# Summed squares on VectorE, value products in pairs of key blocks, and downward blocks by token halves in a two-layer hybrid attention step

## The chip, the core and the metric

The kernel runs on one core of one Trainium2 chip. The metric is the time of one execution on the device in microseconds (us); lower is better. A core has five engines that run their own instruction streams side by side and wait for one another through semaphores: TensorE (PE in the profile, with its weight loads as PEld), VectorE (DVE), ScalarE (ACT), GpSimd (POOL) and SyncE (SP), whose stream here issues the weight transfers.

## The reference

One inference step of two trunk layers with a final norm, on 128 context tokens and 512 latent tokens of width 1024. Cut to what the change touches:

```
def rmsnorm(x, g):
    y = xf * lax.rsqrt(jnp.mean(xf * xf, axis=-1, keepdims=True) + EPS)
    return y * g
...
each layer:
    h   = rmsnorm(x) modulated by adaLN
    z   = h @ w_in                 -> differential, windowed and latent (MLA) heads
    p   = softmax(q k^T)           (context keys, then latent keys)
    mix = p @ v                    for every head
    x  += gate * (mix @ w_out)
    h   = rmsnorm(x) modulated by adaLN
    x  += gate * (relu(h @ w_up)^2 @ w_down)
final rmsnorm
```

The mean of squares of every token over its 1024 channels is what the first part of the change computes in another way; `p @ v` is the second part; the product with w_down the third.

## The kernel before

The activations lie transposed: xT holds 8 chunks of 128 channels by 640 tokens. The tokens go in two halves, HALVES = 0 to 256 and 256 to 640, that is 2 and 3 tiles of 128 (TILES). A product that must be exact is made of three matmuls of split operands, high by high, high by low and low by high (mm3, L540 to L544: lines L542, L543, L544). wh and wl are the high and low parts of a weight tile wr; ACT or DVE makes wh (L399, L414), DVE makes wl as a difference (L407).

The order of nearly all work is set by a planner, the class Plan. The code adds tasks with an engine, an estimated duration, the slots they read, write and allocate, and a priority; Plan schedules them against its own model of the engines (durations tA, tV, tP, hops HOP, ring sizes RINGS, and the settings KP of each layer with a sequence string), and emits each engine's instructions in that order. There are three plans: the attention of layer 0; the attention of layer 1, which begins with the last downward blocks of the MLP of layer 0; and the last downward blocks of layer 1 with the final norm. Between them stands the MLP of a layer, whose order is written out by hand as a list of blocks (L1725 onward): downward blocks ("d", product with w_down) and upward blocks ("u").

RINGS gives the number of buffers of each kind: E (scratch, four), PT (three), t (PSUM, three) matter here. A task that allocates from a full ring waits for the oldest holder's last reader.

The places that the change touches:

- stat(st, k, hf, prio), L639: ScalarE squares chunk k of token half hf into a buffer sq of ring E (L646); PE then multiplies each 128-token tile of it by a column of ones into the PSUM tile st (L651), adding up over the 8 chunks. The trace shows each of these f32 matmuls as two rows. rstd (L656 onward) turns st into the reciprocal root rsq (L611 to L623) and spreads it to all partitions (yb L665, rb L669). One round is all 8 chunks of both halves, 40 matmuls. There are five rounds: at the head of layer 0, in the third part of the output projection of each layer (the product with mix, 'po<-mix', whose residual L735 writes xT), and in the last downward blocks of each layer ('po<-Gt').
- quad(...), L986: two query tiles by two heads of one kind (sw, da, mla). Scores go to PSUM (sps; L1026 for mla), DVE takes the maximum (L1048), ACT the exponential (L1056). Then, per key block: four transposes of the probabilities (tr, L1095) into pt, one copy from PSUM to PT (ACT or DVE, as the planner chooses; lines L399 or L401), and the value product pv (L1099) into O. A value product is two matmuls, one for each head, with 64 columns each, so on half the width of the array.
- the block list, downs(g): for each pair of channel blocks mc two blocks, one for each channel block mi; a block makes the product of its channel block for both token halves, and the residual (L735) follows.
- KP of layer 1 has a key "split" that nothing reads.

pa<-wq,sc (L576) is the product of the conditioning vector with the adaLN weights; asb, pt (L581) its transposed result.

Of the kernel before, what the change touches and what calls it, by code (L numbers as in the profile page):

```python
# [15 lines left out]
ALU = mybir.AluOpType  # L16
# [3 lines left out]
P = 128  # L20
DEPTH = 2
D = 1024
KD = 8
# [4 lines left out]
HALVES = [(0, 256), (256, 640)]  # L28
# [14 lines left out]
N_CST = 900  # L43


RINGS = {"E": 4, "X": 5, "PT": 3, "B": 8, "h": 4, "mix": 3, "quad": 2, "QK": 4, "hs": 2, "wr": 3, "wh": 4, "wl": 4, "zin": 2, "sq4": 2,
         "stt": 10, "osb": 1, "Kc": 1, "ds": 2, "sm": 4, "rsq": 3, "Vsw": 1, "Vda": 1, "Vml": 1, "ckT": 1, "kz": 1,
         "s": 2, "t": 3, "o": 1, "z": 4, "T": 2, "ws": 2}

# [7 lines left out]
DMA0, DMAR = 2.0, 300e3  # L57
WINDOW = 3.413
N_PRE = 2

# [10 lines left out]
     "up_prio": 3500000.0, "split": "V", "evict": 999995.0, "resid": (4, 4, 8, 8), "half": 0.5,  # L71
     "seq": "s1 s0 c1 c2 s1 c1 s1 s1 c1 D0 c1 s0 c1 c1 c1 s0 s0 w1 c1 "
            "w0 d0 c1 D1 V0 c1 c1 c1 d0 d1 M0 d1 c1 w2 m0 m0 M1 m1 m1"},
]
# [7 lines left out]
def tV(n):  # L82
    return 0.07 + n / 960
# [281 lines left out]
def tile_hybrid_step(ctx: ExitStack, tc: tile.TileContext, i, o):  # L365
    nc = tc.nc
    V, S, G, T = nc.vector, nc.scalar, nc.gpsimd, nc.tensor
# [22 lines left out]
    def add(*a, **k):  # L390
        return cur[0].add(*a, **k)
# [43 lines left out]
    def sl(t, table, key):  # L435
# [11 lines left out]
    ones = sl(cst, CST, "ones")  # L447
# [18 lines left out]
                    in1=sil[:, 2].rearrange("p (k s) -> p k s", s=2), op=ALU.mult)  # L466
# [162 lines left out]
    def open_stats(ring, after=()):  # L629
        if ring == "s":  # L630
            x = mk(ring, [P, 2, 512], F32, "st")
            add("V", 0.1, lambda: V.memset(x.t[:, :, 0:4], 0.0), alloc=[x], prio=0.0, after=after)
            return [(x, lambda a, b, hf=hf: x.t[:, hf, a:b]) for hf in range(2)]
        st = [mk(ring, [P, 512], F32, "st") for _ in range(2)]
        for x in st:
            add("V", 0.1, lambda x=x: V.memset(x.t[:, 0:4], 0.0), alloc=[x], prio=0.0, after=after)
        return [(x, lambda a, b, x=x: x.t[:, a:b]) for x in st]

    def stat(st, k, hf, prio):  # L639

        a, b = HALVES[hf]
        w = b - a
        n = TILES[hf][1] - TILES[hf][0]
        x, view = st[hf]
        sq = mk("E", [P, NT], F32, "sq")
        add("A", tA(w) + 0.05, lambda: S.activation(out=sq.t[:, 0:w], in_=xT[:, k, a:b], func=AF.Square),  # L646
            r=[("x", (k, hf))], alloc=[sq], prio=prio)

        def mm():
            for t in range(n):  # L650
                T.matmul(out=view(t, t + 1), lhsT=sq.t[:, t * P:(t + 1) * P], rhs=ones,  # L651
                         start=False, stop=(k == KD - 1), skip_group_check=True)

        add("P", 0.115 * n, mm, r=[sq], w=[(x, hf)], prio=min(prio, 0.9e6))

    def rstd(st, hf, rb, prio):  # L656

# [328 lines left out]
    def quad(l, kind, u, hd, vt, vcols, mix, kt_mix, pr_, hs, at):  # L986
# [98 lines left out]
        ns = len(slots)  # L1085
        O = mk("o", [P, 256], F32, "O")
        p_t = PAR["tr"] + at
        for z, (kt, have) in enumerate(slots):
            pt, PT = mk("t", [P, 2, 256], F32, "pt"), mk("PT", [P, 2, 256], F32, "PT")
            c, w = have[0] * P, len(have) * P  # L1090

            def tr(pt=pt, kt=kt, have=have):
                for x in range(2):
                    for y in have:
                        T.transpose(pt.t[:, x, y * P:(y + 1) * P], e_.t[:, x, y, pos[y][kt]:pos[y][kt] + P], ident)  # L1095

            def pv(z=z, kt=kt, c=c, w=w, PT=PT):
                for x in range(2):
                    T.matmul(out=O.t[64 * x:64 * x + 64, c:c + w], lhsT=vt.t[:, kt, vcols[x]:vcols[x] + 64],  # L1099
                             rhs=PT.t[:, x, c:c + w], start=(z == 0), stop=(z == ns - 1))  # L1100

            add("P", 0.22 * len(have), tr, r=[(e_, (x, y)) for x in range(2) for y in have],
                alloc=[pt], prio=p_t)
            add("AV", {"A": tA(2 * w), "V": tV(2 * w)},
                lambda e, pt=pt, PT=PT, c=c, w=w: copy(e, PT.t[:, :, c:c + w], pt.t[:, :, c:c + w]),
                r=[pt], alloc=[PT], prio=PAR["evict"] + at)
            add("P", 0.255 * len(have), pv, r=[PT, (vt, kt)], w=[] if z == 0 else [O], alloc=[O] if z == 0 else [], prio=p_t,
                narrow=True)
        c0 = P + pr_ * 256
        if kind == "da":  # L1110
            osb = mk("osb", [P, 384], F32, "osb")
# [466 lines left out]
    for l in range(DEPTH + 1):  # L1578
# [134 lines left out]
        with ExitStack() as es:  # L1713
# [16 lines left out]
            def downs(g):  # L1730
                for mc in range(4):
                    if g < 7:
                        blocks.extend(("d", g, mc, mi, len(tiles)) for mi in range(2))
                    raws_.append(["d", g, mc, len(tiles)])
                    tiles.append([("d", g, mc)])

# [85 lines left out]
            for b_, blk in enumerate(blocks):  # L1822
# [1 line left out]
                wh, wl = wt[n_]  # L1824
                now, later = [], []
                if kind == "d":
                    g, mc, mi = f, q, x
                    m = mc * 2 + mi
                    mm_ = slice(mi * P, (mi + 1) * P)
                    whv, wlv = (z.rearrange("p (k n) -> p k n", k=4) for z in (wh, wl))  # L1830
                    for hf in range(2):
                        a0, b0 = HALVES[hf]
                        pu = bank()
                        for k in range(4):
                            gt = Gt[g][k // 2]
                            mm3(pu[:, :b0 - a0], (whv[:, k, mm_], wlv[:, k, mm_]),
                                (gt[:, 0, k % 2, a0:b0], gt[:, 1, k % 2, a0:b0]), k == 0, k == 3)
                        now.append(lambda m=m, hf=hf, pu=pu: emit_resid(l, 5, m, hf, pu))
                else:
                    if f // 4 not in Gt:  # L1840
                        Gt[f // 4] = [sp.tile([P, 2, 2, NT], R, tag="B", name="Gt", bufs=8) for _ in range(2)]
                    gt = Gt[f // 4][(f % 4) // 2]
                    z = {"A11": "X", "A12": "Y", "S2": "X", "S3": "Z", "S1": "X", "A22": "Z", "S4": "X"}[q]
                    new = q in ("A11", "A12", "S3")
                    if new:
                        banks[z] = bank()
                    pu = banks[z][:, 0:320]
                    whv, wlv = (t[:, 512 * x:512 * x + 512].rearrange("p (k n) -> p k n", k=4) for t in (wh, wl))
                    bh, bl = operand(q)
                    out = pu.rearrange("p (t n) -> p t n", n=64)  # L1850
                    for k in range(4):
                        for y, (w_, a_) in enumerate(((whv, bh), (whv, bl), (wlv, bh))):
                            T.matmul(out=out, lhsT=w_[:, k], rhs=a_[:, k], start=new and k == 0 and y == 0,  # L1853
                                     stop=k == 3 and y == 2, skip_group_check=True)
                    if q in ("A11", "S2", "S3"):
                        e = mp.tile([P, 384], F32, tag="X", name="pe", bufs=RINGS["X"])
                        banks["e" + q] = e
                        now.append(lambda e=e, pu=pu: copy(S, e[:, 0:320], pu))
                    else:
# [145 lines left out]
```

## Time and profile before

| | us |
|---|---|
| median of 3 runs | 1760.19 (1755.74 to 1761.95) |
| the profiled execution | 1761.53 |
| its span | 1759.8 |
| granted TensorE clock, mean | 0.984 |

The profile is one execution, read by the engine's rows: each has a start, a duration, the engine, the line, the operation with its output and inputs, and in brackets the idle time before it and what ended it. A busy row of PE can overlap the next, since matmuls are pipelined, so the cost of a stretch is read from start to start. The groups of the profile count the rows of all places of a line. A window view gives the busy time of each engine in a stretch of the span, then the granted clock, the share of the DMA engines and the GB/s. The parts of the program by time: the head to about 60 us, the attention of layer 0 to about 425, its output projection's last part and the entry to the MLP to about 500, the MLP to 870, its last downward blocks to 915; then the same for layer 1, and the final norm from about 1746.

### The profile page before, as it was taken

What the parts mean: (1) busy time and instruction counts of PE and PEld (TensorE: products, weight loads), DVE (VectorE), ACT (ScalarE), POOL (GpSimd) and SP (SyncE); (2) the same over time, 40 slices, a digit from 0 to 9 for tenths busy, and PEclk for the clock granted to TensorE, in tenths of its full rate; (3) what the DMA queues carried; (4) which work ended last, traced back from release to release, by engine and by line L of the source; (5) the groups of instructions that cost most, each with busy time, mean ns of one, the idle gap of its engine ahead of it and who ended that gap; (6) DMA issues with size and microseconds to landing.
All of it is one profiled execution on the core that took longest, in us unless ns stands there. A gap on an engine that the chain in (4) does not pass through costs nothing.

```text
span 1759.8 us, 29841 instructions
## 1 busy us (share of the span) xinstructions
PE 1676.2 (95%) x11335; PEld 1487.5 (85%) x11335; DVE 1242.9 (71%) x3229; ACT 809.5 (46%) x1798; POOL 199.5 (11%) x165
## 2 busy tenths in 40 slices
PE   7899999899899999999999999989889999999997
PEld 6687567568799999999998865857779999999997
DVE  3865778986868667766576767988577867766654
ACT  3532667774525333333254347777353433333321
POOL 0000001100013222212000000300001322212200
PEclk9999999999899999999999999999999999999999
DMA  9322553340122122222213244231111222222121
GB/s 314 102 84 87 200 165 96 108 139 25 61 70 87 61 87 82 97 85 77 89 52 98 88 135 137 90 108 56 36 61 50 71 93 76 96 88 70 61 73 61
DMA packets 67391, 163.24 MB, mean 93 GB/s; under 512 B 6896, under 2 KB 31280, under 8 KB 67248
## 3 DMA queue, kind: packets, MB, share of 16 engines
q1 hardware_dynamic: 67248, 161.34, 28.3%
q8 instruction: 90, 1.47, 0.3%
q14 instruction: 53, 0.43, 0.1%
HBM read 153.15 MB, written 8.16 MB: 92 GB/s over the span
## 4 chain that ended last, share of the span: by engine, by line
PE 79%; DVE 10%; ACT 4%; DMA 2%; issue 1%; POOL 1%; SPq 0%; DVEq 0%; ACTq 0%; POOLq 0%
PE pu L1853 18%; PE pu L543 8%; PE pu L542 8%; PE pu L544 8%; PE pt L1095 3%; PE O L1099 3%; PE po L542 3%; PE po L544 3%; PE pz L830 3%; PE pz L832 3%; PE po L543 3%; PE pz L831 3%; PE sps L1026 2%; PE st L651 2%; DMA zin<-zda 2%
## 5 line engine op out<-in xcount | busy, mean ns | idle before, releaser
L407 DVE TENSOR_TENSOR wl<-wr,wh 128x512 fp32r<-128x512 f32 (+2 forms) x290 | 287.0, 1010 | 62.0 <-ACT wh L414 37.4
L399 ACT ACTIVATE wh<-wr 128x512 fp32r<-128x512 f32 (+1 forms) x228 | 161.0, 736 | 282.6 <-PE pu L543 176.3
L542 PE MATMUL pu<-Gt,wh 128*128 128x384 f32 (+1 forms) x896 | 277.7, 310 | 5.1 <-DVE r L1449 5.1
L543 PE MATMUL pu<-Gt,wh 128*128 128x384 f32 (+1 forms) x896 | 277.6, 310 | 0.0
L544 PE MATMUL pu<-Gt,wl 128*128 128x384 f32 (+1 forms) x896 | 277.6, 310 | 0.0
L735 DVE SCALAR_TENSOR_TENSOR xT<-pu,ada,xT 128x128 f32<-128x128 f32 x336 | 134.8, 434 | 146.0 <-PE pu L544 145.7
L542 PEld LDWEIGHTS pu<-Gt,wh 128*128 128x128 f32 x896 | 170.6, 190 | 5.7 <-DVE r L1449 5.7
L543 PEld LDWEIGHTS pu<-Gt,wh 128*128 128x128 f32 x896 | 170.6, 190 | 0.0
L544 PEld LDWEIGHTS pu<-Gt,wl 128*128 128x128 f32 x896 | 170.5, 190 | 0.0
L1853 PE MATMUL pu<-Tl,wh 128*128 128x320 f32 x448 | 138.0, 308 | 0.0
L1853 PE MATMUL pu<-Th,wl 128*128 128x320 f32 x448 | 138.0, 308 | 0.0
L1853 PE MATMUL pu<-Th,wh 128*128 128x320 f32 x448 | 138.0, 308 | 0.0
L830 PE MATMUL pz<-wh,hh 128*128 128x512 f32 (+1 forms) x320 | 128.3, 401 | 2.1 <-DVE m L763 1.0
L831 PE MATMUL pz<-wl,hh 128*128 128x512 f32 (+1 forms) x320 | 123.4, 386 | 2.6 <-DVE wl L407 2.6
L735 DVE SCALAR_TENSOR_TENSOR xT<-po,ada,xT 128x128 f32<-128x128 f32 (+1 forms) x192 | 77.0, 434 | 66.3 <-PE po L544 65.2
L832 PE MATMUL pz<-wh,hl 128*128 128x512 f32 (+1 forms) x320 | 123.7, 386 | 0.1
L1048 DVE TENSOR_REDUCE stt<-sps 128x1 f32<-128x640 f32 (+2 forms) x160 | 116.1, 737 | 9.1 <-PE sps L1041 5.0
L1853 PE MATMUL pu<-hh,wh 128*128 128x320 f32 x336 | 104.2, 310 | 4.6 <-DVE r L1868 4.6
L1056 ACT ACTIVATE quad<-sps,stt 128x640 f32<-128x640 f32 (+2 forms) x128 | 91.2, 713 | 27.5 <-DVE stt L1048 26.9
L1853 PE MATMUL pu<-hh,wl 128*128 128x320 f32 x336 | 103.8, 309 | 0.0
L1853 PE MATMUL pu<-hl,wh 128*128 128x320 f32 x336 | 103.6, 308 | 0.0
L1427 POOL TENSOR_TENSOR xT<-xT,tm 128x256 f32<-128x256 f32 (+1 forms) x32 | 30.1, 941 | 619.8 <-ACT tm L1423 365.3
(313 smaller groups left out, 3930.7 us busy)
## 6 DMA issues: line engine op xcount, KB each, us to landing
wr<-in_w_ada SPq DMA_DIRECT2D x80, 512.0 KB, 3.8
wr<-in_w_up SPq DMA_DIRECT2D x64, 512.0 KB, 3.5
wr<-in_w_down SPq DMA_DIRECT2D x64, 512.0 KB, 3.5
wr<-in_w_in SPq DMA_DIRECT2D x24, 512.0 KB, 3.5
wr<-in_w_out SPq DMA_DIRECT2D x16, 512.0 KB, 4.5
wq<-in_w_ada SPq DMA_DIRECT2D x6, 1024.0 KB, 6.9
wr<-in_w_in SPq DMA_DIRECT2D x8, 416.0 KB, 3.4
xT<-in_xT SPq DMA_DIRECT2D x4, 640.0 KB, 7.1
```

The costliest lines, as they stand in the source:

```text
L399: S.activation(out=out, in_=in_, func=AF.Copy)
L407: eng.tensor_tensor(out=out, in0=a, in1=b, op=ALU.subtract)
L542: T.matmul(out=out, lhsT=w[0], rhs=a[0], start=first, stop=False)
L543: T.matmul(out=out, lhsT=w[0], rhs=a[1], start=False, stop=False)
L544: T.matmul(out=out, lhsT=w[1], rhs=a[0], start=False, stop=last)
L735: V.scalar_tensor_tensor(out=xT[:, m, a:b], in0=po[:, a - a0:b - a0], scalar=ada[l][:, sec, m, s:s + 1], in1=xT[:, m, a:b], op0=ALU.mult, ...
L830: T.matmul(out=out, lhsT=h_at(h, "h", k, tk), rhs=wh[:, x], start=(k == 0), stop=False)
L831: T.matmul(out=out, lhsT=h_at(h, "h", k, tk), rhs=wl[:, x], start=False, stop=False)
L832: T.matmul(out=out, lhsT=h_at(h, "l", k, tk), rhs=wh[:, x], start=False, stop=(k == KD - 1))
L1048: add("V", tV(we) - 0.01, lambda st=st, j=j, view=view: V.tensor_reduce(out=st.t[:, j:j + 1], in_=view(), axis=AX.X if kind == "sw" else A ...
L1056: S.activation(out=out, in_=view(), func=AF.Exp, bias=st.t[:, j:j + 1], accum_out=st.t[:, 4 + j:5 + j])
L1853: T.matmul(out=out, lhsT=w_[:, k], rhs=a_[:, k], start=new and k == 0 and y == 0, stop=k == 3 and y == 2, skip_group_check=True)
```

## The change

Four edits, in a kernel that is otherwise the same:

1. Summed squares: the squares of chunks 0 to 6 are added up by DVE in the buffer of chunk 0 (six adds per half and round), and PE multiplies by ones only that sum and the square of chunk 7: 10 matmuls a round in place of 40.
2. Value products: the transposes and copies of N_PV = 2 key blocks go first, then their value products as one task. Ring PT has four buffers in place of three. Five key blocks make groups of 2, 2 and 1.
3. Downward blocks by token halves: a block holds both channel blocks of a pair for one token half, in place of one channel block for both halves.
4. The unread key "split" goes.

```diff
-RINGS = {"E": 4, "X": 5, "PT": 3, ...
+RINGS = {"E": 4, "X": 5, "PT": 4, ...
...
+N_PV = 2
...
     def stat(st, k, hf, prio):
...
-        x, view = st[hf]
+        x, view, part = st[hf]
         sq = mk("E", [P, NT], F32, "sq")
         add("A", tA(w) + 0.05, lambda: S.activation(out=sq.t[:, 0:w], in_=xT[:, k, a:b], func=AF.Square),
             r=[("x", (k, hf))], alloc=[sq], prio=prio)
+        if k == 0:
+            part.append(sq)
+        elif k < KD - 1:
+            acc = part[0]
+            add("V", tV(w), lambda: V.tensor_tensor(out=acc.t[:, 0:w], in0=acc.t[:, 0:w], in1=sq.t[:, 0:w], op=ALU.add),
+                r=[sq], w=[acc], prio=prio)
+        if k < KD - 2:
+            return
+        src = part[0] if k < KD - 1 else sq
 
         def mm():
             for t in range(n):
-                T.matmul(out=view(t, t + 1), lhsT=sq.t[:, t * P:(t + 1) * P], rhs=ones,
+                T.matmul(out=view(t, t + 1), lhsT=src.t[:, t * P:(t + 1) * P], rhs=ones,
                          start=False, stop=(k == KD - 1), skip_group_check=True)
...
+            pvs.append((kt, c, w, PT))
+            if len(pvs) < N_PV and kt != slots[-1][0]:
+                continue
+
+            def pv(pvs=pvs, z0=z0, O=O):
+                for z, (kt, c, w, PT) in enumerate(pvs):
+                    for x in range(2):
+                        T.matmul(out=O.t[64 * x:64 * x + 64, c:c + w], lhsT=vt.t[:, kt, vcols[x]:vcols[x] + 64],
+                                 rhs=PT.t[:, x, c:c + w], start=(z0 + z == 0), stop=(z0 + z == ns - 1))
...
-                        blocks.extend(("d", g, mc, mi, len(tiles)) for mi in range(2))
+                        blocks.extend(("d", g, mc, hf, len(tiles)) for hf in range(2))
...
-                    g, mc, mi = f, q, x
-                    m = mc * 2 + mi
-                    mm_ = slice(mi * P, (mi + 1) * P)
+                    g, mc, hf = f, q, x
+                    a0, b0 = HALVES[hf]
...
-                    for hf in range(2):
-                        a0, b0 = HALVES[hf]
+                    for mi in range(2):
+                        m = mc * 2 + mi
+                        mm_ = slice(mi * P, (mi + 1) * P)
```

Since the planner works from the tasks, the order moves all over its three parts. Line numbers of the changed kernel are higher by 1 (helpers) to 19. Three places:

PE, the first instructions of the program, before; st is the sum of squares, pa the product with the conditioning vector, pt its transpose:

```order
L651 MATMUL st<-cst,sq 128x1 x37
L576 MATMUL pa<-wq,sc 32x128 x8
L651 MATMUL st<-cst,sq 128x1 x3
L581 MATMUL pt<-cst,asb 128x128
L576 MATMUL pa<-wq,sc 32x128 x8
```

and the same place of the changed kernel:

```order
L662 MATMUL st<-cst,sq 128x1 x10
L577 MATMUL pa<-wq,sc 32x128 x16
L680 MATMUL rb<-cst,yb 128x128 x2
L582 MATMUL pt<-cst,asb 128x128 x2
L577 MATMUL pa<-wq,sc 32x128 x8
```

All statistics now stand ahead of the first product with the conditioning vector, and the spread reciprocal root (rb) of the first half is two runs earlier.

PE, in the attention of layer 1, one group of latent attention (mla) before; quad are the probabilities, sps scores, spc scores of context queries:

```order
L1095 MATMUL pt<-cst,quad 128x128 x8
L1026 MATMUL sps<-Kml,Qml 128x320 x6
L1099 MATMUL O<-PT,Vml 64x256 x4
L1095 MATMUL pt<-cst,quad 128x128 x8
L1169 MATMUL spc<-Kcml,Qml 128x128 x6
L1099 MATMUL O<-PT,Vml 64x256 x4
L1095 MATMUL pt<-cst,quad 128x128 x4
```

and a group of the same kind in the changed kernel:

```order
L1107 MATMUL pt<-cst,quad 128x128 x8
L1037 MATMUL sps<-Kml,Qml 128x320 x6
L1107 MATMUL pt<-cst,quad 128x128 x4
L1121 MATMUL O<-PT,Vml 64x256 x4
L1107 MATMUL pt<-cst,quad 128x128 x8
L1037 MATMUL sps<-Kml,Qml 128x320 x6
L1121 MATMUL O<-PT,Vml 64x256 x6
```

Five key blocks have value products in runs of two and three blocks, with transposes of three blocks ahead of them; over the whole program the runs of value products on PE go from 90 to 53.

DVE, at the entry to the MLP of layer 0, before; Tl is the last sum of the normed tokens, r and Gt the first upward results, wl the low half of a downward weight tile, xT the residual of the first downward blocks:

```order
L407 TENSOR_TENSOR Tl<-hs,Th 128x4x384 x2
L407 TENSOR_TENSOR wl<-wr,wh 128x1024
L1449 SCALAR_TENSOR_TENSOR r<-pu,r 128x384 x4
L407 TENSOR_TENSOR Gt<-r,Gt 128x384 x4
L407 TENSOR_TENSOR wl<-wr,wh 128x1024 x3
L735 SCALAR_TENSOR_TENSOR xT<-pu,ada_92,xT 128x128 x2
```

and after:

```order
L408 TENSOR_TENSOR Tl<-hs,Th 128x4x384 x2
L1468 SCALAR_TENSOR_TENSOR r<-pu,r 128x384 x4
L408 TENSOR_TENSOR Gt<-r,Gt 128x384 x4
L408 TENSOR_TENSOR wl<-wr,wh 128x1024 x4
L746 SCALAR_TENSOR_TENSOR xT<-pu,ada_92,xT 128x128 x4
L746 SCALAR_TENSOR_TENSOR xT<-pu,ada_92,xT 128x384 x2
```

The first low half has moved behind the first upward results, and the residual goes by token halves.

More of the change, by code (lines that the diff above doesn't have):

```diff
@@ L43 @@
 N_CST = 900
-RINGS = {"E": 4, "X": 5, "PT": 3, "B": 8, "h": 4, "mix": 3, "quad": 2, "QK": 4, "hs": 2, "wr": 3, "wh": 4, "wl": 4, "zin": 2, "sq4": 2,
+RINGS = {"E": 4, "X": 5, "PT": 4, "B": 8, "h": 4, "mix": 3, "quad": 2, "QK": 4, "hs": 2, "wr": 3, "wh": 4, "wl": 4, "zin": 2, "sq4": 2,
          "stt": 10, "osb": 1, "Kc": 1, "ds": 2, "sm": 4, "rsq": 3, "Vsw": 1, "Vda": 1, "Vml": 1, "ckT": 1, "kz": 1,
@@ L70 @@
      "out": ("AV", "V"), "scale": "AV", "lead": 30, "prep": 950000.0, "tr": 900000.0, "up": ("A", "V"),
-     "up_prio": 3500000.0, "split": "V", "evict": 999995.0, "resid": (4, 4, 8, 8), "half": 0.5,
+     "up_prio": 3500000.0, "evict": 999995.0, "resid": (4, 4, 8, 8), "half": 0.5,
      "seq": "s1 s0 c1 c2 s1 c1 s1 s1 c1 D0 c1 s0 c1 c1 c1 s0 s0 w1 c1 "
@@ L632, in open_stats @@
             add("V", 0.1, lambda: V.memset(x.t[:, :, 0:4], 0.0), alloc=[x], prio=0.0, after=after)
-            return [(x, lambda a, b, hf=hf: x.t[:, hf, a:b]) for hf in range(2)]
+            return [(x, lambda a, b, hf=hf: x.t[:, hf, a:b], []) for hf in range(2)]
         st = [mk(ring, [P, 512], F32, "st") for _ in range(2)]
@@ L636, in open_stats @@
             add("V", 0.1, lambda x=x: V.memset(x.t[:, 0:4], 0.0), alloc=[x], prio=0.0, after=after)
-        return [(x, lambda a, b, x=x: x.t[:, a:b]) for x in st]
+        return [(x, lambda a, b, x=x: x.t[:, a:b], []) for x in st]
     def stat(st, k, hf, prio):
@@ L647, in stat @@
             r=[("x", (k, hf))], alloc=[sq], prio=prio)
+        if k == 0:
[7 more added lines that the diff above has]
+        src = part[0] if k < KD - 1 else sq
         def mm():
             for t in range(n):
-                T.matmul(out=view(t, t + 1), lhsT=sq.t[:, t * P:(t + 1) * P], rhs=ones,
+                T.matmul(out=view(t, t + 1), lhsT=src.t[:, t * P:(t + 1) * P], rhs=ones,
                          start=False, stop=(k == KD - 1), skip_group_check=True)
-        add("P", 0.115 * n, mm, r=[sq], w=[(x, hf)], prio=min(prio, 0.9e6))
+        add("P", 0.115 * n, mm, r=[src], w=[(x, hf)], prio=min(prio, 0.9e6))
     def rstd(st, hf, rb, prio):
@@ L1087, in quad @@
         p_t = PAR["tr"] + at
-        for z, (kt, have) in enumerate(slots):
+        z0, pvs = 0, []
+        for kt, have in slots:
             pt, PT = mk("t", [P, 2, 256], F32, "pt"), mk("PT", [P, 2, 256], F32, "PT")
@@ L1095, in tr @@
                         T.transpose(pt.t[:, x, y * P:(y + 1) * P], e_.t[:, x, y, pos[y][kt]:pos[y][kt] + P], ident)
[L1097 to L1100, printed above, removed]
             add("P", 0.22 * len(have), tr, r=[(e_, (x, y)) for x in range(2) for y in have],
@@ L1106, in quad @@
                 r=[pt], alloc=[PT], prio=PAR["evict"] + at)
-            add("P", 0.255 * len(have), pv, r=[PT, (vt, kt)], w=[] if z == 0 else [O], alloc=[O] if z == 0 else [], prio=p_t,
-                narrow=True)
+            pvs.append((kt, c, w, PT))
[6 more added lines that the diff above has]
+                                 rhs=PT.t[:, x, c:c + w], start=(z0 + z == 0), stop=(z0 + z == ns - 1))
+            add("P", 0.255 * sum(w // P for _, _, w, _ in pvs), pv,
+                r=[q for kt, _, _, PT in pvs for q in (PT, (vt, kt))], w=[] if z0 == 0 else [O],
+                alloc=[O] if z0 == 0 else [], prio=p_t, narrow=True)
+            z0, pvs = z0 + len(pvs), []
         c0 = P + pr_ * 256
```

## The prediction

> **What bounds the kernel now.** I read the page first: the busy shares, then the chain that ended last.
>
> ```profile
> span 1759.8 us, 29841 instructions
> ...
> PE 1676.2 (95%) x11335; PEld 1487.5 (85%) x11335; DVE 1242.9 (71%) x3229; ACT 809.5 (46%) x1798; POOL 199.5 (11%) x165
> ...
> PE 79%; DVE 10%; ACT 4%; DMA 2%; issue 1%; POOL 1%; SPq 0%; DVEq 0%; ACTq 0%; POOLq 0%
> ```
>
> TensorE (PE) is busy for 95% of the span and carries 79% of the chain. PE time that goes is mostly time that goes, unless another engine is late at that place. So I cut the span into stages; the columns are PE, weight load, VectorE, ScalarE and GpSimd busy us, then the granted clock.
>
> ```profile
> core 0: us, PE busy (x) PEld busy (x) DVE busy (x) ACT busy (x) POOL busy (x), PEclk, DMA share, GB/s
> ...
> 150.00:430.00 280.00, 263.34 (x1986) 187.56 (x1984) 206.64 (x587) 178.82 (x442) 17.46 (x24) 0.99 0.39 121
> ...
> 550.00:870.00 320.00, 320.00 (x2190) 320.00 (x2189) 218.69 (x394) 112.43 (x206) 61.98 (x43) 1.00 0.26 86
> 870.00:915.00 45.00, 45.00 (x302) 43.22 (x301) 28.37 (x87) 20.23 (x44) 0.00 (x0) 1.00 0.21 60
> ...
> 1713.00:1760.00 47.00, 36.90 (x270) 36.34 (x269) 22.38 (x69) 7.55 (x16) 0.00 (x0) 0.91 0.16 57
> ```
>
> In layer 0 the attention (150:430) has PE at 94%, the MLP (550:870) and the last downward blocks with the statistics of the next norm (870:915) have PE at 100% while VectorE has 32% and 37% of slack. Layer 1 repeats these stages, and 1713:1760 is its last downward stage and the tail.
>
> **The change part by part. 1, summed squares in the last downward stages.** A round (five tiles by eight chunks, 40 matmuls, each shown as two rows) falls to 10 matmuls, and there are five rounds, so the 400 rows of this group become 100.
>
> ```profile
> L651 PE MATMUL st<-cst,sq 128*128 128x1 f32 x400 | 57.0, 261 | 8.0 <-ACT sq L646 8.0
> ```
>
> What a set costs is read from start to start, since ends overlap.
>
> ```profile
> 878.01 0.50 PE L651 MATMUL st<-cst,sq 128*128 128x1 f32 x4
> 878.38 0.36 PE L542 MATMUL po<-Gt,wh 128*128 128x256 f32 x1
> 878.58 0.28 PE L543 MATMUL po<-Gt,wh 128*128 128x256 f32 x1
> 878.69 0.28 PE L544 MATMUL po<-Gt,wl 128*128 128x256 f32 x1
> ...
> 886.83 0.72 PE L651 MATMUL st<-cst,sq 128*128 128x1 f32 x6
> 887.41 0.42 PE L542 MATMUL po<-Gt,wh 128*128 128x384 f32 x1
> ```
>
> A set of two tiles holds PE for 0.37 us, and the product behind it is followed after 0.20 instead of 0.11: 0.46 us. Three tiles: 0.58 + 0.09 = 0.67. Six of eight sets go in each half: 6 x (0.46 + 0.67) = 6.8 us a round. In these two stages PE has no gap, so all of it counts: 2 x 6.8 = **-13.5 us**. [...]
>
> VectorE gains 6 adds per half. It has the same form, two f32 operands in SBUF, in these rows:
>
> ```profile
> 449.89 0.42 DVE L407 TENSOR_TENSOR hl<-hs,hh 128x256 fp32r<-128x256 f32 x1
> ...
> 471.72 0.55 DVE L407 TENSOR_TENSOR hl<-hs,hh 128x384 fp32r<-128x384 f32 x1
> ```
>
> 6 x (0.42 + 0.55) = 5.8 us a round. In 870:915 VectorE has 45.0 - 28.4 = 16.6 us free, which hides them. Without that cover they would be 11.6 us in the two stages, and the term would be -1.9. Bounds: -13.5 and -2.
>
> **2, the head.** The same sets stand at the very start.
>
> ```profile
> 7.58 15.95 PE L651 MATMUL st<-cst,sq 128*128 128x1 f32 x74 [7.58 <-ACT sq L646]
> 23.45 1.08 PE L576 MATMUL pa<-wq,sc 128*32 128x128 f32 x16
> 24.46 1.44 PE L651 MATMUL st<-cst,sq 128*128 128x1 f32 x6
> 25.77 0.45 PE L581 MATMUL pt<-cst,asb 128*128 128x128 f32 x1
> ```
>
> The waits of the first 60 us (total us, times, longest), and a window of the same stretch:
>
> ```profile
> DVE rsq L611 <- PE st L651: 20.8, 2, 19.5
> ...
> 32.00:40.00 8.00, 7.80 (x49) 4.74 (x50) 4.65 (x17) 2.79 (x7) 0.00 (x0) 1.00 0.92 310
> ```
>
> 80 rows end at 25.8, 0.215 us each (the first 74 in 15.95), and the reciprocal root (rsq) waits for them 19.5 us. After, 20 rows cost 4.3 us, and the squares set the pace: 16 squares and 12 adds in turns. ScalarE alone needs 16 x 0.47 = 7.5 us from 7.1, to 14.6; squares and adds strictly in turn need 7.5 + 5.8 more, to 20.4; ring E has four places, of which the two sums hold two. I take 18. PE then has 8 us less in front of the projections. But up to 40 us the transfers run at 92% or more, and the wq loads on SP's queue wait for the pa products that are moved forward; what PE does at 33 cannot all come 8 us sooner. I take **-5**, between 0 (transfers bind) and -10.
>
> **3, the two output projections.** Their third parts run at 425:448 and 1268:1291.
>
> ```profile
> 440.00:448.00 8.00, 8.00 (x60) 8.00 (x60) 4.51 (x15) 3.56 (x6) 0.00 (x0) 1.00 0.21 68
> 448.00:456.00 8.00, 7.71 (x61) 5.91 (x59) 7.97 (x24) 7.56 (x21) 0.00 (x0) 1.00 0.37 131
> ...
> 464.00:472.00 8.00, 2.58 (x10) 1.51 (x10) 5.85 (x17) 4.66 (x11) 0.00 (x0) 0.75 0.00 1
> 472.00:480.00 8.00, 7.75 (x30) 7.68 (x30) 8.00 (x16) 5.49 (x11) 0.00 (x0) 0.61 0.01 2
> ```
>
> To 448 PE is full and VectorE has 44% free; from 448 VectorE is full and PE stands for 5.4 us of 464:472. The first piece would give 6.8 us. But the 5.8 us of adds come just ahead of a stretch in which VectorE binds, and behind an add wait the residual of the next block, the normed halves (hs, hl) and PE's upward products. I take **-3 a stage, -6** in all; bounds -6.8 and +5.8 a stage, so -13.6 and +11.6.
>
> **4, value products two key blocks at a time.** The matmuls stay; what goes is changes between full and half width of the array.
>
> ```profile
> 395.98 1.05 PE L1026 MATMUL sps<-Kml,Qml 96*128 96x320 f32 x6
> 396.86 1.04 PE L1095 MATMUL pt<-cst,quad 128*128 128x128 f32 x8
> ...
> 400.57 1.12 PE L1026 MATMUL sps<-Kml,Qml 96*128 96x320 f32 x6
> 401.62 1.08 PE L1099 MATMUL O<-PT,Vml 128*64 128x256 f32 x8
> 402.63 0.66 PE L1095 MATMUL pt<-cst,quad 128*128 128x128 f32 x4
> ...
> 404.33 0.65 PE L1099 MATMUL O<-PT,Vml 128*64 128x256 f32 x4
> 404.91 0.45 PE L542 MATMUL po<-mix,wh 128*128 128x384 f32 x1
> ```
>
> Into the run: six scores hold PE 0.88 us ahead of transposes, 1.05 ahead of a value product, 0.17 more. Out: four rows take 0.58, eight 1.01, so 0.43 for four and 0.15 fixed. One trip costs 0.32 us. By the order of the instructions PE makes 53 such runs instead of 90: 37 x 0.32 = 11.8 us. The price is a wait: the first block's evicted copy now waits for the second's.
>
> ```profile
> L399 ACT ACTIVATE PT<-pt 128x512 f32<-128x512 f32 (+1 forms) x91 | 51.1, 575 | 31.9 <-PE pt L1095 29.2 <-PE O L1099 2.0
> ```
>
> An eviction takes 0.58 us, and PE can go on only with what stands between. In the new order mostly other work stands there (six scores, 0.9 us, or products), and ring PT has a fourth place, so that two pairs are under way. Priced with such rows, 20 of 144 gaps between a last transpose and its value product were shorter than 1.2 us before, and 6 are now. The planner also reorders the whole stage: ten value evictions go from VectorE to ScalarE, and some scalings to VectorE. PE has 17 us of gaps in 150:430 that may grow or shrink; I bound this reshuffle at +20 over both layers. I take **-9**, bounds -12 and +8.
>
> **5, downward blocks by halves, and the entry to the MLP.** A block has the same 24 matmuls with four forms in another order; PE at 100% in 550:870 does the same work, so 0. At the entry of layer 0 the order changes.
>
> ```profile
> 491.14 1.23 DVE L407 TENSOR_TENSOR wl<-wr,wh 128x1024 fp32r<-128x1024 f32 x1 [3.13 <-ACT wh L414]
> 492.29 1.94 DVE L1449 SCALAR_TENSOR_TENSOR r<-pu,r 128x384 f32<-128x384 f32 x4
> 494.15 1.95 DVE L407 TENSOR_TENSOR Gt<-r,Gt 128x384 fp32r<-128x384 f32 x4
> ...
> 494.28 0.39 PE L542 MATMUL pu<-Gt,wh 128*128 128x256 f32 x1 [2.54 <-DVE r L1449]
> ```
>
> Before, the low half of the first weight (wl) was made ahead of r and Gt. After, it stands behind both on VectorE: 491.1 + 1.9 + 1.9 + 1.2 = 496.1 if r starts at once, and up to 497.3 if not, and PE's third matmul needs it, which before could go at about 494.7, right behind the last row and the one after it. That is +1.6 to +2.8; I take +2.6. In layer 1 the order stays and the first products need one token half only: 0 to -2, I take -1. Sum **+1.6**.
>
> **The sum.** -13.5 - 5 - 6 - 9 + 1.6 = -31.9 on the profiled execution's 1761.5: 1729.6. That execution is 1.3 above the median, so 1728. Bounds: all at best -13.5 - 10 - 13.6 - 12 - 0.4 = -49.5, 1711; all at worst -1.9 + 0 + 11.6 + 8 + 2.8 = +20.5, 1781, which needs every cover to fail at once.
>
> **Rivals.** *VectorE takes PE's place* in the head and in the output projections: the adds there are as long as the sets (5.8 against 6.8). For it: 7.97 of 8 us busy at 448:456. Against it: 44% free just before. Then the stages give 0 and the head 0: -13.5 - 9 + 1.6 = -21, and with +3 a stage -15: 1742 to 1745.
>
> *PE falls to half rate more often.* In 472:480, behind a gap of 5.4 us, the granted clock is 0.61. With sets of matmuls gone, PE is left with gaps. Such a fall costs 8 x (1 - 0.61) = 3.1 us; four more (each output projection, the head, the start of an attention) cost 12.4: 1728 + 12 = 1740. Against it: where the most matmuls go, PE is gapless. [...]
>
> *The change doesn't do what it says:* the planner spends the PE time that goes in gaps elsewhere, and the total stays at 1755 to 1765. Against it: 13.5 us lie where PE has no gap.
>
> *Slower: value products wait for the second eviction.* Place: transposes and value products of both attentions. If less than 0.9 us of PE work stands between the last transpose of a pair and its products, PE waits out the hop and the 0.58 us. At 80 pairs of four-row transposes, 80 x 0.6 = 48 us, against savings of 33: +15, 1775. It decides from 55 such pairs on (33/0.6); the order shows 6 short gaps, but evictions that stand behind other work on ScalarE or VectorE would count too.
>
> **How the numbers follow.** Forecast 0.70 (1728, own range 1716 to 1738); VectorE in PE's place 0.12 (1742 to 1745); half rate 0.10 (1740); no change 0.04 (1760); slower 0.04 (1775). The range takes the forecast's lower bound, 1711, and reaches to 1749 over both middle rivals. A measurement of this kernel tells 0.3% (5.3 us) from no change. Faster 0.92, same 0.04, slower 0.04.
>
> **What would show each step.** 1: 100 rows of st<-cst,sq, the last downward stages 6 to 7 us shorter with PE still at 100%; a wait of PE on adds there refutes it. 2: the wait of rsq on st down from 19.5 to about 12, PE's projections 5 us sooner. 3: the span from the last part of the output projection to the first upward product 3 us shorter, and no more than 8 us idle behind it. 4: 37 fewer runs of value products, PE waits on PT not above the 6 or so us of before. 5: PE's first downward product at layer 0 waits on wl. The forecast is wrong if PE's total falls by 25 us or more but the span does not.

## The result and the profile after

The changed kernel takes 1709.63 us (median of 4 runs, 1707.87 to 1710.98) against 1759.93 before (4 runs): a ratio of 0.9717, 95% interval 0.9696 to 0.9737, so 50.3 us less. The forecast was 1728 with a range from 1711 to 1749: the sign was right, the size too small by 18 us, and the range missed the time by 1.4 us. Medians and ratios here and below leave out two executions, one of pairs with three buffers and one of the kernel before in another order (j3), which took 2684 and 2690 us at a granted clock of 0.56.

The profiled execution took 1707.87 us, 53.7 less than that of before; it lies 1.8 below its median, that of before 1.6 above. The page of the changed kernel, the lines that answer to those of before:

```profile
span 1706.1 us, 29317 instructions
...
PE 1617.0 (95%) x11035; PEld 1446.2 (85%) x11035; DVE 1276.6 (75%) x3293; ACT 801.9 (47%) x1792; POOL 203.8 (12%) x167
...
PE 75%; DVE 14%; ACT 5%; DMA 2%; issue 2%; POOL 1%; DVEq 0%; SPq 0%; ACTq 0%; POOLq 0%
```

PE is busy 59 us less at the same share of the span, and VectorE's share of the last chain went from 10% to 14%. To see where the time went, I cut both traces at the same points of the program, read off PE's rows: the first product of each input projection (pz), the first upward block of each MLP that reads the token sums (Tl, Th), and the first of the last downward blocks (po<-Gt). The windows view of before, the seven stages in order (head, attention 0, MLP 0, last downward 0, attention 1, MLP 1, last downward 1; an attention stage includes the output projection and the entry to the MLP):

```profile
0.00:33.61 33.61, 23.99 (x152) 20.86 (x153) 8.85 (x47) 12.70 (x27) 0.20 (x4) 1.00 0.97 330
33.61:527.56 493.95, 462.38 (x3141) 361.72 (x3138) 360.93 (x1139) 271.53 (x650) 25.50 (x30) 0.98 0.34 106
527.56:867.62 340.06, 338.05 (x2307) 337.52 (x2306) 237.01 (x414) 122.41 (x228) 74.44 (x50) 1.00 0.25 85
867.62:904.10 36.48, 36.48 (x269) 36.48 (x269) 22.90 (x66) 17.86 (x39) 0.00 (x0) 1.00 0.13 38
904.10:1371.01 466.91, 438.91 (x2896) 355.67 (x2896) 351.01 (x1081) 253.92 (x610) 25.20 (x31) 0.97 0.27 85
1371.01:1711.60 340.59, 338.04 (x2306) 337.52 (x2305) 238.87 (x414) 122.47 (x228) 74.15 (x50) 1.00 0.23 79
1711.60:1753.17 41.57, 38.30 (x278) 37.74 (x277) 20.05 (x62) 8.61 (x17) 0.00 (x0) 0.98 0.11 39
```

and of the changed kernel:

```profile
0.00:24.76 24.76, 10.64 (x93) 8.45 (x94) 13.80 (x57) 11.93 (x28) 0.20 (x4) 1.00 0.99 329
24.76:503.49 478.73, 445.59 (x3077) 355.19 (x3077) 370.46 (x1159) 266.51 (x644) 25.34 (x30) 0.98 0.35 116
503.49:843.84 340.35, 338.21 (x2307) 337.69 (x2305) 238.92 (x414) 122.48 (x228) 74.63 (x50) 1.00 0.25 85
843.84:873.13 29.29, 29.29 (x203) 29.25 (x203) 23.93 (x70) 16.06 (x35) 0.93 (x2) 1.00 0.11 33
873.13:1320.63 447.50, 421.66 (x2841) 345.39 (x2840) 361.19 (x1099) 253.69 (x614) 28.56 (x31) 0.99 0.29 90
1320.63:1662.92 342.29, 339.75 (x2306) 339.22 (x2305) 239.85 (x414) 122.58 (x228) 74.14 (x50) 1.00 0.23 78
1662.92:1699.47 36.55, 31.83 (x218) 30.99 (x217) 25.23 (x74) 8.61 (x17) 0.00 (x0) 0.96 0.12 43
```

The second number is the stage's length, the third PE's busy time. Head -8.9; last downward stages -7.2 and -5.0; MLPs +0.3 and +1.7; the two attention stages **-15.2 and -19.4**. The forecast had -5, -13.5 together, 0, and -13.4 for both attention stages. So the error lies mostly in the attention stages: 34.6 us where 13.4 were forecast.

A stage's length has three parts: gaps (length less PE's busy time), what PE loses to the granted clock (busy time by one less the clock, summed over windows of 1 us; called half rate below), and the rest, its **work** in full-speed time. The windows view gives a clock of 1.00 also where the trace has no record of it, and the record begins only at 37.9 us in before and at 23.8 in the changed kernel. By its rows, PE ran at about half speed ahead of it: the first projection rows of before follow one another at 0.43 us, and those behind 38 us at 0.23.

```profile
34.20 0.63 PE L831 MATMUL pz<-wl,hh 128*128 128x512 f32 x1
34.63 0.63 PE L832 MATMUL pz<-wh,hl 128*128 128x512 f32 x1
...
39.96 0.39 PE L830 MATMUL pz<-wh,hh 128*128 128x512 f32 x1
40.19 0.39 PE L831 MATMUL pz<-wl,hh 128*128 128x512 f32 x1
```

So I take a clock of 0.5 up to the first record, an estimate from these rows. By the view alone the attention stages of before would have 2.1 us more work and as much less half rate; it is 1.0 to 2.1 in the other runs whose head keeps its 40 matmuls, and nothing in the rest. For the two attention stages together: work 879.1 to 856.5, **-22.6**; half rate 22.2 to 10.8, **-11.4**; gaps 59.6 to 59.0, -0.6. The work that left is closer to the undiscounted prices of the prediction, 2 x 6.8 for the sums and 11.8 for the pairs, 25.4, than to the 15 that it counted. The rest is less time at half rate, which the prediction had counted as 0. Each split is of one execution: those of the kernel before beside the last set lay between 1752.7 us at a granted clock of 0.990 and 1761.8 at 0.984, so a few us of half rate belong to the execution.

### The profile page after: what moved, and what is told of

It is laid out like the page before. It is cut to its first block, busy times and chain, and to the rows that moved or that the text cites. A ratio compares the mean times of both kernels' runs of the same rounds, so it can differ in the third digit from the quotient of the medians.

```text
span 1706.1 us, 29317 instructions
## 1 busy us (share of the span) xinstructions
PE 1617.0 (95%) x11035; PEld 1446.2 (85%) x11035; DVE 1276.6 (75%) x3293; ACT 801.9 (47%) x1792; POOL 203.8 (12%) x167
## 4 chain that ended last, share of the span: by engine, by line
PE 75%; DVE 14%; ACT 5%; DMA 2%; issue 2%; POOL 1%; DVEq 0%; SPq 0%; ACTq 0%; POOLq 0%
PE pu L1872 18%; PE pu L545 8%; PE pu L544 8%; PE pu L543 8%; PE pt L1107 3%; PE po L543 3%; PE pz L841 3%; PE O L1121 3%; PE pz L842 3%; PE pz L843 3%; PE po L544 3%; PE po L545 3%; DVE stt L1059 2%; DVE wl L408 2%; DMA zin<-zda 1%
## 5 line engine op out<-in xcount | busy, mean ns | idle before, releaser
L408 DVE TENSOR_TENSOR wl<-wr,wh 128x512 fp32r<-128x512 f32 (+2 forms) x290 | 291.6, 1027 | 55.5 <-ACT wh L415 31.0
L408 DVE TENSOR_TENSOR Gt<-r,Gt 128x320 fp32r<-128x320 f32 (+2 forms) x128 | 79.0, 624 | 25.2 <-ACT Gt L400 25.2
L408 POOL TENSOR_TENSOR wr<-wr 128x512 f32<-128x512 f32 x28 | 39.4, 1407 | 486.0 <-DMA wr<-in_w_up 345.2
## 6 DMA issues: line engine op xcount, KB each, us to landing
wq<-in_w_ada SPq DMA_DIRECT2D x6, 1024.0 KB, 12.1
```

Source lines behind the costliest of these rows:

```text
L408: eng.tensor_tensor(out=out, in0=a, in1=b, op=ALU.subtract)
```

## The experiments

Theories: **A**, prices: each matmul and each change of array width that leaves PE counts in full. **B**, VectorE binds in the output projections, and what went beyond the forecast comes from the planner's new order. **C**, the fourth PT buffer, not the pairs, makes the second part. The times below are medians; the kernel before, run beside each set, had 1757.8, 1758.1, 1758.0 and 1756.1, so a comparison across sets is good to some 4 us. Orders of one kernel, shown last, differ by up to 6 us in work, so a smaller difference of work tells nothing by itself.

### The parts alone

The summed squares alone: the stat hunk of the diff on the kernel before.

```diff
+            add("V", tV(w), lambda: V.tensor_tensor(out=acc.t[:, 0:w], in0=acc.t[:, 0:w], in1=sq.t[:, 0:w], op=ALU.add),
```

> The summed squares alone, on the kernel before. Theory A (prices add up: every set of sums that leaves PE counts in full, in the head, in both output projections and in both last downward stages): head -9, output projections 2 x -6.8, last downward stages 2 x -6.8, some -36 us, about 1724. Theory B (the extra gain of the changed kernel comes from the planner's new order, which needs the pairs of value products or their fourth buffer): head -9, downward stages -13, output projections near -3 each, about 1732. The entry to the attention stages decides: from the first product of the input projection to the first upward block of the MLP, -6.8 a layer by A, about -3 a layer by B.

Measured 1716.9, ratio 0.9766 (0.9751 to 0.9780), -40.9. More than either theory. Work in the attention stages fell by 14.6 (A: 13.6), gaps and half rate by 10.3.

The pairs alone: the quad hunks with N_PV = 2 and PT at 4.

```diff
-"PT": 3
+"PT": 4
...
+N_PV = 2
...
```

> Value products of two key blocks and the fourth PT buffer alone, on the kernel before. Runs of value products on PE fall from 92 to 53. Theory A (0.32 us a trip, no waits): -12 us, 1748, all in the two attention stages. Theory B (the new order of the whole stage brings more than the trips): -20 us or more. Theory C (it does nothing without the relief of PE and VectorE by the other part): within 5 us of before.

Measured 1738.7, ratio 0.9894 (0.9879 to 0.9908), -19.2. Work in the attention stages fell by 11.2 (A: 12), gaps by 3.0, half rate by 8.0. The price of a trip was about right, and the time moved by more, nearly as far as B has it. The trace of before has 92 runs of value products, not the 90 counted ahead of the prediction: 39 trips less, 12.5 us by the price.

The downward blocks by halves alone:

```diff
-blocks.extend(("d", g, mc, mi, len(tiles)) for mi in range(2))
+blocks.extend(("d", g, mc, hf, len(tiles)) for hf in range(2))
...
```

> Downward blocks by token halves alone, on the kernel before. All theories: the MLP blocks cost the same; A expects 0 to -3 us at the two entries to the MLP, B allows for -5 and more where the first half's block no longer waits for the second half's upward results.

Measured 1758.3, ratio 1.0006 (0.9992 to 1.0019): nothing, work unchanged at 879.1.

The two parts together, without the third (the hunks of both, downs as before):

```diff
+N_PV = 2
...
+            add("V", tV(w), lambda: V.tensor_tensor(out=acc.t[:, 0:w], in0=acc.t[:, 0:w], in1=sq.t[:, 0:w], op=ALU.add),
...
```

> Summed squares and pairs of value products without the downward blocks by halves. A: -36 - 12 = -48, about 1712, the changed kernel less than 3 us faster. B: the parts don't add up, and this differs from the sum of the two single parts by more than 6 us.

Measured 1708.9, ratio 0.9730 (0.9713 to 0.9746), -48.9, the changed kernel's time. The single parts sum to -60.1, 11.2 more, so in time they don't add up. By work in the attention stages they nearly do, 14.6 + 11.2 = 25.8 against 22.1, a difference that orders alone can make; gaps and half rate don't: 10.3 + 11.0 = 21.3 against 11.2.

### The output projections

The sums everywhere but in the output projections:

```diff
...
-                        stat(sts, m, hf_, 0.2e6 + m)
+                        stat(sts, m, hf_, 0.2e6 + m, each=True)
```

> The kernel before with the summed squares in the head and in the last downward stages only; the third part of both output projections keeps 40 matmuls a round. Against the run with summed squares everywhere (-41 us), the difference is the term of the output projections. Theory A (each set that leaves PE counts in full there too): 13.6 us and what the half-rate spells of PE change with it, so -41 + 14 = -27, about 1731. Theory B (VectorE takes PE's place there, as the prediction's discount has it): 6 us, -35, about 1723.

Measured 1742.4, ratio 0.9912 (0.9892 to 0.9932). Against the sums everywhere it is 25.4 us slower: work 15.8 more in the attention stages, gaps 5.6, half rate 3.6. A's 13.6 is near the work; the time moved by more than either theory says. The stretch itself, from the start of the last third of the output projection's products to the first block that reads the token sums, in the two layers without the sums there:

```profile
407.80:513.42 105.62, 96.03 (x641) 91.03 (x640) 77.66 (x170) 42.87 (x83) 8.50 (x6) 0.97 0.16 53
1241.86:1358.08 116.22, 103.36 (x669) 95.86 (x668) 77.80 (x174) 45.47 (x86) 7.94 (x6) 0.94 0.16 52
```

and with them:

```profile
405.95:502.69 96.74, 89.87 (x585) 85.37 (x584) 81.74 (x183) 41.92 (x82) 8.51 (x6) 0.95 0.18 58
1227.76:1332.26 104.50, 95.04 (x618) 88.79 (x616) 80.90 (x183) 44.27 (x85) 7.80 (x6) 0.95 0.18 59
```

It is 8.9 and 11.7 us shorter, and its gaps fall too, from 9.6 to 6.9 and from 12.9 to 9.5. The discount to 3 a stage was wrong.

Is VectorE idle there, then? Every add doubled by another that writes a dead buffer, in the same order:

```diff
+                V.tensor_tensor(out=sq.t[:, 0:w], in0=sq.t[:, 0:w], in1=sq.t[:, 0:w], op=ALU.add)
```

> The changed kernel with every add of squares followed by a second one of the same size into a buffer that nothing reads any more; the order on all engines is that of the changed kernel, with 60 adds more on VectorE (5.8 us a round, 29 in all). Theory A (the adds are hidden beside PE in the output projections and in the downward stages): at most +6 us, nearly all of it in the head, where squares and adds go in turn. Theory B (VectorE is the bound in the output projections): +5.8 in each of them, so +12 to +18 in all.

Measured 1731.1, ratio 0.9855 (0.9841 to 0.9870), 21.5 above the changed kernel: some three quarters of the 29 us of adds come through. In the output projections and the entries (from the last value product to the first block behind the entry) they cost 4.3 and 5.7 us, in the head 4.6, in the last downward stages 3.4 and 3.5; the other attention rows shift by gaps and half rate both ways. So a second add is not hidden, and the first was still worth it. This alone doesn't show a full VectorE: in the last downward stage of layer 0 VectorE is busy for 26.5 of 33 us (850:883 of this run) and the adds cost 3.4 all the same, since PE waits 0.4 us for the longer chain of adds and 0.8 us for a late square, and falls to half rate behind them (granted clock 0.95 from 850.1 to 882.8). That VectorE is near its limit in the output projection, the windows of the changed kernel around its first one show (third busy number, of 8 us):

```profile
412.00:420.00 8.00, 8.00 (x58) 8.00 (x58) 6.44 (x21) 2.74 (x7) 0.00 (x0) 1.00 0.00 1
420.00:428.00 8.00, 7.65 (x55) 6.19 (x55) 7.93 (x17) 5.17 (x10) 0.00 (x0) 1.00 0.30 100
428.00:436.00 8.00, 4.97 (x24) 4.36 (x24) 7.86 (x35) 6.24 (x16) 0.00 (x0) 0.63 0.42 165
436.00:444.00 8.00, 8.00 (x65) 7.91 (x64) 7.82 (x17) 2.67 (x6) 0.00 (x0) 0.95 0.23 68
```

From 420 on VectorE is full, and PE nearly so until 428: the adds used up what had been free.

Some adds off VectorE again, those of chunks 1 to 5 of these two rounds on GpSimd:

```diff
+            gp = pool and k < KD - 2
+            add("G" if gp else "V", tG(w) if gp else tV(w), lambda e=G if gp else V: e.tensor_tensor(
...
```

> The changed kernel with the adds of chunks 1 to 5 on GpSimd in the third part of both output projections (20 adds off VectorE). Doubling all adds cost 21 us, some 4 to 6 of them in each output projection, so VectorE is close to the bound there now. If it is the bound, and GpSimd is free: -3 to -4 us a stage, -6 to -8 in all. If the adds on GpSimd (about 1 us each by the residual adds it does elsewhere) come late, or the two engines block one another: 0 to +10.

Measured 1707.9, ratio 0.9712 (0.9691 to 0.9734): no difference from the changed kernel that can be told (expected, if VectorE binds there and GpSimd is free: -6 to -8), and another order, so it doesn't say what the adds themselves cost.

### Pairs or buffers

The fourth buffer alone:

```diff
-"PT": 3
+"PT": 4
```

> The kernel before with four PT buffers in place of three, value products still one key block at a time. By the order, runs of value products on PE fall from 92 to 79. Trips alone (0.32 us each): -4 us. If the buffer, and not the pairs, is what the second part brings: -15 us or more of the -19 that the pairs with four buffers gave.

Measured 1751.1, ratio 0.9962 (0.9950 to 0.9973), -7.0; work -5.3 for 13 trips less (4.2 by the price).

Pairs with three buffers:

```diff
+N_PV = 2
...
```

> The kernel before with value products of two key blocks, but with three PT buffers. Runs of value products 64 by the order, where four buffers gave 53 and one block at a time 92. Trips alone: 28 x 0.32 = -9 us. If pairs need the fourth buffer, since a pair holds two of three until its products are done: not faster than before, with PE waits on PT.

Measured 1764.6, ratio 1.0032 (1.0017 to 1.0048): slower, though its work fell by 6.2. Gaps and half rate rose by 9.5. Of PE's waits (total us, times, longest) those for evictions hardly grew, from 3.0 us in before to some 4, 3.4 of them of transposes whose PSUM buffer ScalarE has not emptied yet, and none of value products. What grew are transposes of queries and keys that wait for VectorE (pt<-sq, from 3.9) and scores that wait for an exponential (sps<-e, from 1.7), so in this trace the pair itself isn't what waits (the first line is as in before):

```profile
PE rb L670 <- DVE yb L666: 9.7, 4, 2.8
PE pt L1274 <- DVE sq L408: 8.6, 9, 2.3
...
PE sps L1019 <- ACT e L1057: 5.9, 8, 1.2
...
PE pt L1097 <- ACT PT L400: 3.4, 6, 0.7
```

Three key blocks at a time, six buffers, on the changed kernel:

```diff
-"PT": 4
+"PT": 6
...
-N_PV = 2
+N_PV = 3
```

> The changed kernel with value products of three key blocks at a time and six PT buffers. Runs of value products on PE: 45, where the changed kernel has 53. Trips alone: 8 x 0.32 = -2.6 us. If waits for evictions are what limits, slower than the changed kernel by 3 us and more; if the order that the planner finds matters more than the trips, off by more than 4 us either way.

Measured 1718.3, ratio 0.9783 (0.9766 to 0.9800): 8.7 slower than the changed kernel, with 2.5 us less work, as the 8 trips say, 3.4 us more gaps and 12.1 us more at half rate. C falls: of the 19.2 us the buffer alone brings 7.0, and pairs without it lose 6.6. In the last two runs gaps and half rate decide more than the trips.

### The same work in another order

If the order decides, it can be changed without the work. One estimate of the planner moved by 0.01 us, in both kernels:

```diff
-"PA": 0.2,
+"PA": 0.21,
```

> The kernel before, with one estimate of the planner moved by 0.01 us (the hop from PE to ScalarE, 0.20 to 0.21). The work is the same; only the order differs. If the order by itself is worth little (the gain beyond the prices belongs to the change): within 4 us of before. If it is luck of the order: 5 us and more either way, in the time PE loses to half rate and in its gaps, with its work within 3 us.

> The changed kernel with the same estimate moved. If the gain beyond the prices belongs to the change: within 4 us of the changed kernel. If it is luck of the order: slower by 5 us and more (the changed kernel has the least time at half rate of all kernels so far, 10.7 us in the two attention stages), so about 1715 to 1720.

Before: 1761.2, ratio 1.0021 (1.0009 to 1.0032). After: **1743.7**, ratio 0.9921 (0.9896 to 0.9947), 34 us slower than the changed kernel. Its attention stages, in the windows view:

```profile
24.77:521.38 496.61, 456.32 (x3078) 361.36 (x3077) 379.30 (x1181) 261.03 (x622) 24.92 (x30) 0.96 0.34 112
...
890.98:1353.99 463.01, 428.78 (x2840) 350.39 (x2840) 365.34 (x1109) 251.64 (x604) 28.23 (x31) 0.98 0.28 87
```

17.9 and 15.5 us longer, with 2.6 us more work, 15.5 us more gaps and 15.2 us more at half rate in the two together. Two more orders of each, with the same estimate at 0.19 (j2) and with the hop from VectorE to PE at 0.24 for 0.23 (j3):

```diff
-"PA": 0.2,
+"PA": 0.19,
...
-"VP": 0.23
+"VP": 0.24
```

> The kernel before with the planner's hop from PE to ScalarE at 0.19 in place of 0.20. Same work, another order. If its order is an ordinary draw: within 5 us of before. If gaps and half rate vary as they did for the changed kernel (31 us): up to 20 us off either way.

> The kernel before with the hop from VectorE to PE at 0.24 in place of 0.23. As for the other moved estimate: within 5 us of before, or up to 20 us off.

> The changed kernel with the hop from PE to ScalarE at 0.19. PE's work in the attention stages within 3 us of the changed kernel's 856. If its 70 us of gaps and half rate are a lucky draw: slower by 5 to 30 us. If the first moved estimate (+34 us) was the unlucky one: within 5 us.

> The changed kernel with the hop from VectorE to PE at 0.24. Work within 3 us of 856; slower by 5 to 30 us if its order is a lucky draw, within 5 us if not. The mean over the changed kernel's four orders against the mean over the four of before is the gain that the work explains, some -40 to -46 us, if order is independent of the change.

| order | time, us | work | gaps | half rate |
|---|---|---|---|---|
| before | 1759.9 | 879.1 | 59.6 | 22.2 |
| before, 0.21 | 1761.2 | 872.7 | 63.0 | 22.3 |
| before, j2 | 1759.9 | 878.4 | 59.2 | 20.9 |
| before, j3 | 1756.4 | 876.8 | 59.3 | 20.1 |
| changed | 1709.6 | 856.5 | 59.0 | 10.8 |
| changed, 0.21 | 1743.7 | 859.1 | 74.5 | 26.0 |
| changed, j2 | 1712.7 | 854.7 | 63.6 | 16.4 |
| changed, j3 | 1705.0 | 855.8 | 58.4 | 11.6 |

(work, gaps and half rate of the two attention stages together.) Work divides the kernels cleanly: 872.7 to 879.1 before, 854.7 to 859.1 after, 20.3 apart on average. Gaps and half rate together average 81.6 before and 80.1 after, but lie within 79.4 to 85.3 before and 69.7 to 100.5 after. Over the four orders each, the mean times differ by 41.6 us, about half of it work of the attention stages and most of the rest the head and the last downward stages; the changed kernel's own order is one of the good ones. Four orders that lie 39 us apart fix the changed kernel's mean only roughly. The ratios of j3, 0.9708 (0.9691 to 0.9725), and of the changed kernel overlap, so it isn't shown to be faster.

## Why the prediction was right or wrong

**1, last downward stages: right in the sum, not in every sign.** Forecast -13.5, measured -12.2: -7.2 with PE still full, and -5.0. The second stage was not gapless before, as the prediction has it (PE busy 38.3 of 41.6 us), and in it PE ends up waiting 1.6 us for an add ahead of the final sums, the wait that by the prediction would refute the step. The cover of 16.6 us did not say that: free time of an engine hides work only where nobody waits for its last piece.

```profile
1694.58 1.05 PE L662 MATMUL st<-cst,sq 128*128 128x1 f32 x8 [1.57 <-DVE sq L654]
```

**2, the head: right in its mechanism, too small.** The sums end where I put them (18):

```profile
13.55 4.42 PE L662 MATMUL st<-cst,sq 128*128 128x1 f32 x20 [13.55 <-DVE sq L654]
17.90 1.93 PE L577 MATMUL pa<-wq,sc 128*32 128x128 f32 x32
```

and all of the 8 us came: -8.9. The transfers, still near saturation (0.99 of the engines' time to 24.8 us), did not hold the projections back. The wait of rsq fell to 2.4 us and not to 12, because PE now does the waiting, 13.5 us from the start, for the adds.

**3, the output projections: the step that failed.** "I take -3 a stage, -6 in all", because the adds come just ahead of a stretch in which VectorE binds. By the runs with and without the sums there, a stage gains 8.9 and 11.7 us: the sets left PE in full (15.8 us of work), and the gaps did not grow for it. The wait on VectorE that the discount was for did come, but in place of another one. Before, PE goes from the last projection product to the first upward product in 1.3 us without a gap and then waits for the second half:

```profile
468.43 0.87 PE L669 MATMUL rb<-cst,yb 128*128 128x128 f32 x3 [2.82 <-DVE yb L665]
471.42 0.66 PE L542 MATMUL pu<-hh,wh 128*128 128x384 f32 x1 [2.12 <-DVE hh L401]
```

After, it waits ahead of the first upward product:

```profile
429.45 0.44 PE L680 MATMUL rb<-cst,yb 128*128 128x128 f32 x2 [0.85 <-DVE yb L676]
...
431.97 0.58 PE L1482 MATMUL pu<-hh,wh 128*128 128x256 f32 x1 [2.08 <-DVE hh L402]
```

Gaps ahead of that product are 3.2 and 4.6 us where there were none; from there to the first block that reads the token sums they are 6.0 and 0.6 where they were 9.0 in both layers.

**4, pairs: right in mechanism and nearly in price; the reshuffle was mis-sized.** -9 forecast, out of 11.8; the work of the pairs alone is 11.2. The waits view of the changed kernel has no wait of a value product for an eviction (before: 1.4 us), so the slower rival didn't come. The reshuffle was bounded at a loss of 20 and taken as 0; in this order gaps and half rate fell by 12.0 us, in another of the same work they rose by 19. That they fell here is luck: over the four orders each they differ by 1.6.

**5, halves and the entry: the wait came, the sum nearly.** Alone the halves change nothing. In layer 0 PE waits for wl as described:

```profile
466.36 0.39 PE L543 MATMUL pu<-Gt,wh 128*128 128x256 f32 x1 [1.69 <-DVE r L1468]
466.59 0.28 PE L544 MATMUL pu<-Gt,wh 128*128 128x256 f32 x1
470.10 0.58 PE L545 MATMUL pu<-Gt,wl 128*128 128x256 f32 x1 [3.23 <-DVE wl L408]
```

The wait is 3.2 us, with PE at half rate behind it (granted clock 0.60 in 468:476; it was 1.00 in 476:484). From the first downward product to the first block that reads the token sums, the stretch grew by 3.8 us in layer 0 (2.6 forecast) and fell by 0.9 in layer 1 (1 forecast). In layer 0 the same wait is in the run without the halves, where the entry is as long, so it belongs to the reordering by the other parts.

**The rivals.** VectorE in PE's place: not at this amount of adds (its price of -21 gives 1739, not 1742). Half rate more often: the other way here (-11.4), though it is half of what makes the order with 0.21 slow. The gap of 5.4 us on which this rival rests is several waits, none longer than the 2.8 us shown above. The last term, of order, is what the range lacked on the good side. By terms of the span: head 3.9 beyond the forecast, downward stages 1.3 short, MLPs 2.0 short, attention work 9.2 beyond (-22.6 against -13.4), gaps and half rate 12.0 beyond: together 21.8, from -31.9 to -53.7. So two terms failed: the discount of part 3 by a wrong reading of VectorE, and the reshuffle, put at nothing, by the luck of one order. The mean of the four orders, 1717.8, lies inside the range.

## What to carry to other kernels

Where an engine is full, price what leaves it in full, and discount only by a wait that you can name row by row; a neighbour that has slack may carry new work once and not twice: here the first add was worth its place, and a second was not hidden. Where a planner sets the order, judge an edit by the work that it moves and by several orders of the same work, since one order can carry 10 us of luck in a difference of 42. Look at the parts of a stage apart (work, gaps, clock): only the first came near its forecast here.

## What the runs showed of the hardware

In the changed kernel with the moved estimate (0.21), the granted clock fell to half behind a window in which PE was busy for 6.5 of 8 us. The record of the clock falls at 352.6 us. The windows up to there and behind:

```profile
344.00:352.00 8.00, 6.54 (x51) 3.61 (x52) 6.33 (x18) 6.14 (x17) 0.30 (x2) 1.00 0.75 220
352.00:353.00 1.00, 1.00 (x8) 0.90 (x7) 1.00 (x6) 0.98 (x3) 0.00 (x0) 0.82 0.74 287
353.00:354.00 1.00, 1.00 (x5) 0.71 (x4) 1.00 (x5) 1.00 (x2) 0.00 (x0) 0.50 0.14 57
...
360.00:370.00 10.00, 9.83 (x52) 7.82 (x50) 8.48 (x24) 6.91 (x17) 0.00 (x0) 0.51 0.44 146
370.00:380.00 10.00, 10.00 (x80) 7.27 (x78) 5.51 (x15) 5.48 (x12) 0.00 (x0) 1.00 0.27 106
```

```profile
349.91 0.44 PE L582 MATMUL pt<-cst,asb 128*128 128x128 f32 x2 [0.51 <-ACT asb L400]
...
357.04 3.56 PE L1037 MATMUL sps<-Kml,Qml 96*128 96x320 f32 x12 [2.32 <-ACT e L1067]
...
361.42 1.97 PE L1037 MATMUL sps<-Kml,Qml 96*128 96x320 f32 x6
```

The longest wait of PE in the rows from 349.9 us to the fall is the 0.51 us shown; the one of 2.3 us lies inside the spell. PE then works 9.8 of 10 us at a granted clock of 0.51 (six scores take 1.97 us; at full rate they took 1.05 in the rows of before).

From its first record to the end of the MLP of layer 1 the clock stands at 0.50 for 47.8 us in all in the profiled execution of before, with PE busy for 40.2 of them, and for 34.1 us in that of the changed kernel, with PE busy for 24.6.

The sums' rows of the changed kernel take 0.22 us each in the head (20 in 4.42), but 0.10 in its last downward stage of layer 1, where the granted clock is 1.00 (six in the 0.59 us from 1681.77 to the next row). The head lies ahead of the first record of the clock, where the projection rows of before follow one another at 0.43 us and behind it at 0.23. By that ratio, an estimate, half rate would account for most of the difference; no record shows the clock there, and what is left stays open.
